# A sixth tile over VectorE and DRAM, and the norm weights moved ahead of the root, in a hybrid decoder layer

## The chip, the cores and the metric

The kernel runs on one core of one Trainium2 chip. The metric is the device time of one execution in microseconds; the kernel before took 946.97 us (median of three runs, 946.80 to 948.84). A profile is one execution recorded by the hardware; its times are us from the first instruction.

## The reference

One decoder layer over 1024 tokens of width 1024 (16 learned tokens go ahead of them and are dropped at the end), all in fp32:

```python
u = rmsnorm(h, g_pre_mix)
q, k, v, xr, yr = split(u @ w_in)
attn = sliding_window_attention_with_sinks(q, k, v, sinks)      # window 128
rec = gelu(yr) * rg_lru(causal_depthwise_conv(xr), ...)
h = h + rmsnorm(concat([attn, rec]) @ w_out, g_post_mix)        # first residual
u = rmsnorm(h, g_pre_ffn)                                       # second norm
f = square(relu(u @ w_ff1)) @ w_ff2                             # width 4096 inside
h = h + rmsnorm(f, g_post_ffn)
# rmsnorm(x, g) = x * rsqrt(mean(x * x) + 1e-6) * g
```

The change touches the two lines from the out-projection's norm to the second norm.

## The kernel before, in words

Every fp32 product is made of three matmuls: each operand is split into a high part, rounded to TensorE's fp32r format, and a low part, the rest (`split`: ScalarE casts, L96, VectorE subtracts, L99), and `mm3` (L125, L130, L131) adds high x high, high x low and low x high in a PSUM bank. The two products of the feed-forward part are done by a seven-product block scheme on halves of tokens, rows and columns, so that sums and differences of the normed rows (`t_sums`, `t_rest`) and of the weights (`prep_a`) are made beforehand on VectorE (`combine`, L1124).

The **out-projection** works on eight tiles of 128 tokens. `out_mm` adds eight chunks (`kc`) of 128 rows of `w_out` into two banks of 512 columns for each tile. For tiles 0 to 3 chunks 0 to 3 come first, then 4 and 5, then 6 and 7 tile by tile; tiles 4 to 7 run whole. After each tile `out_norm` does the first norm and residual:

- ScalarE squares both banks with a running sum (L1055) into `h` as scratch; VectorE adds the sums (L172), GpSimd takes the power -1/2 (L176): the root `rs`.
- VectorE multiplies each bank by `rs` and the weights `gmix_b` into `h` (L1061), then adds the residual `xr` (L1064). `h` goes to `out` (L1065).
- ScalarE squares `h` into `xr` as scratch (L1067), and GpSimd makes the second root `rs2`.

The second norm's rows must stand transposed, with features on the partitions, in the tiles `u2f` (`c` in the trace). There are two ways, and `MOVED` divides them:

- **Tiles below `MOVED`** (0 to 4): `u2_store` multiplies `h` by `rs2` and the weights `gpre_b`, reading both with a step of four elements so that the columns are "dealt" into four groups (L1011), transposes blocks of 32 x 32 on VectorE (L1018), and stores the tile to DRAM (L1019; `u_dram` in the trace). `u2_read` brings it back in four DMAs with the rows in place (L1023).
- **Tiles from `MOVED` on** (5 to 7): `out_scale` multiplies by `rs2` (ScalarE, L1081; tile 7 VectorE, L1079), and `u2_tiles` transposes eight blocks on TensorE against the identity (L1093) into two PSUM banks of tag `o`; ScalarE writes them to `u2f` times the norm weight by partition (L1110; half of tile 7 on VectorE, L1101).

Behind tile 7 TensorE goes straight on with the first products of the feed-forward part: `p1` and `p2` on tiles 0 to 3, then those that need all eight tiles (`ot2`, made by `t_sums`). `t_sums` is called three times: for tiles 4 and 5 (`slice(0, 8)`), then 6, then 7.

Buffers go by tags with a fixed count: `raw` 2 (`h`, early weights), `e` 2 (`gmix_b`, the transposed `y`, some weights), `d` 4 (`xr`), `ws` 5 (`gpre_b`, weights). A new user waits until the last one of a buffer is done. The order of instructions in each engine's queue is made by a scheduler that goes by program order as priority and by its own estimate of when operands and buffers are ready; `behind(a, b)` pins single instructions. Each queue, SyncE's DMA queue too, is worked off in order.

Of the kernel before, what the change touches and what calls it, by code (L numbers as in the profile page):

```python
# [11 lines left out]
AF = mybir.ActivationFunctionType  # L12
ALU = mybir.AluOpType
# [3 lines left out]
P = 128  # L17
D = 1024
# [19 lines left out]
def hybrid_layer(  # L38
# [6 lines left out]
    nc = tc.nc  # L45
# [12 lines left out]
    def slot(tag, shape, dt=F32):  # L58
        uid[0] += 1
        return slab.tile(shape, dt, tag=tag, name=f"{tag}{uid[0]}", bufs=bufs[tag])  # L60
# [20 lines left out]
    def lut(*args, **kwargs):  # L81
        ins = nc.scalar.activation(*args, **kwargs).ins
        if last_lut[0] is not None:
            tc.add_manual_dep(
                ins, last_lut[0],
                mybir.DependencyInfo(
                    mybir.DependencyClass.NoSync, mybir.DependencyReason.DATA
                ),
                reason="lut",
            )  # L90
        last_lut[0] = ins.name
        return ins
# [13 lines left out]
    def behind(name, *inss):  # L106
        for ins in inss:
            tc.add_manual_dep(
                ins, name,
                mybir.DependencyInfo(  # L110
                    mybir.DependencyClass.NoSync, mybir.DependencyReason.DATA
                ),
                reason="order",
            )
# [52 lines left out]
    def rstd_of(ssq_parts, n=P):  # L167
        ms = small.tile([P, 1], F32, name="ms", tag="ms")
        if len(ssq_parts) == 1:
            nc.gpsimd.tensor_scalar(ms[:n], ssq_parts[0], EPS, None, op0=ALU.add)  # L170
        else:
            nc.vector.scalar_tensor_tensor(  # L172
                ms[:n], ssq_parts[0], EPS, ssq_parts[1], op0=ALU.add, op1=ALU.add
            )
        rs = small.tile([P, 1], F32, name="rs", tag="rs")
        last_pow[0] = nc.gpsimd.tensor_tensor(  # L176
            rs[:n], ms[:n], half_pow[:n], op=ALU.pow
        ).ins.name
        return rs[:n]
# [50 lines left out]
    RMS_SC = 1.0 / math.sqrt(D)  # L230
# [744 lines left out]
    for half in range(2):  # L975
        for c in range(NLRU):
            y = ys[c][:, 512 * half : 512 * half + 512]
            ins = lut(y, y, AF.Gelu_apprx_tanh)
# [18 lines left out]
    gmix_b = slot("e", [P, D])  # L997
    nc.scalar.dma_start(gmix_b, g_post_mix[0].partition_broadcast(P))
    t4_dram = dpool.tile([P, 2, 4, 512], F32, name="t4_dram")

    MOVED = 5
    u2f = [[slot("c", [P, 16, 2, 32]) for _ in range(4)] for _ in range(2)]
    u2_dram = dpool.tile([MOVED, 4, P, 2 * P], F32, name="u2_dram")
    gpre_b = slot("ws", [P, D])
    nc.scalar.dma_start(gpre_b, g_pre_ffn[0].partition_broadcast(P))

    def dealt(t_):
        return t_.rearrange("p (n b) -> p b n", b=4)

    def u2_store(t, h, rs, tmp):  # L1010
        ins = nc.vector.scalar_tensor_tensor(  # L1011
            tmp.rearrange("p (b n) -> p b n", b=4), dealt(h), rs,
            dealt(gpre_b), op0=ALU.mult, op1=ALU.mult,
        ).ins
        if t < 3:
            behind(summed[t + 1], ins)
        y = slot("e", [P, D])
        nc.vector.transpose(y, tmp)  # L1018
        nc.sync.dma_start(u2_dram[t].rearrange("a (d b) r -> (a d) (b r)", b=4), y)  # L1019

    def u2_read(t):
        for q in range(4):
            nc.sync.dma_start(  # L1023
                u2f[t // 4][q][:, 4 * (t % 4) : 4 * (t % 4) + 4].rearrange(
                    "p a k t -> p a (k t)"
                ),
                u2_dram[t, :, :, 64 * q : 64 * q + 64].rearrange("a p r -> p a r"),
            )

    def out_mm(t, po, kcs):  # L1030
        half, o = t // 4, (t % 4) * P
        s = slice(o, o + P)
        for n in range(2):
            c = slice(512 * n, 512 * n + 512)
            for kc in kcs:
                ah, al = at[half][kc // 2]
                mm3(
                    po[n], (ah[:, kc % 2, s], al[:, kc % 2, s]),
                    (wo[kc][0][:, c], wo[kc][1][:, c]), kc == 0, kc == KC - 1,
                )  # L1040

    def out_banks(t):
        tag = ("pt", "o", "acc", "s", "pt", "acc", "s", "pt")[t]
        return [bank(tag), bank(tag)]

    summed = {}

    def out_norm(t, po):
        xr = slot("d", [P, D])
        nc.sync.dma_start(xr, x[t * P : (t + 1) * P, :])  # L1050
        h = slot("raw", [P, D])
        ssq = [small.tile([P, 1], F32, name=f"sq{n}", tag=f"sq{n}") for n in range(2)]
        for n in range(2):
            c = slice(512 * n, 512 * n + 512)
            nc.scalar.activation(  # L1055
                h[:, c], po[n], AF.Square, scale=RMS_SC, accum_out=ssq[n]
            )
        rs = rstd_of(ssq)
        for n in range(2):
            c = slice(512 * n, 512 * n + 512)  # L1060
            nc.vector.scalar_tensor_tensor(  # L1061
                h[:, c], po[n], rs, gmix_b[:, c], op0=ALU.mult, op1=ALU.mult
            )
        summed[t] = nc.vector.tensor_tensor(h, h, xr, op=ALU.add).ins.name  # L1064
        nc.sync.dma_start(out[t * P : (t + 1) * P, :], h)  # L1065
        ssq2 = small.tile([P, 1], F32, name="ssq", tag="ssq")
        squared[0] = nc.scalar.activation(  # L1067
            xr, h, AF.Square, scale=RMS_SC, accum_out=ssq2
        ).ins.name
        return h, xr, rstd_of([ssq2])  # L1070
# [3 lines left out]
    def out_scale(t, h, xr, rs2):  # L1074
        if t < MOVED:
            u2_store(t, h, rs2, xr)
            return None
        if t == 7:
            nc.vector.tensor_scalar(xr, h, rs2, None, op0=ALU.mult)  # L1079
        else:  # L1080
            nc.scalar.activation(xr, h, AF.Copy, scale=rs2)  # L1081
        return xr
# [4 lines left out]
    def u2_tiles(t, xn):  # L1087
        o = 4 * (t % 4)
        for k4 in range(0, KC, 4):
            pt = bank("o", (P, 4, P))  # L1090
            for i in range(4):
                kc = k4 + i
                turned[0] = nc.tensor.transpose(  # L1093
                    pt[:, i, :], xn[:, kc * P : (kc + 1) * P], ident
                ).ins.name
            pt = pt.rearrange("p k (a t) -> p k a t", t=32)
            for i in range(0, 4, 2):
                kc = k4 + i
                dst = by_k(u2f[1][kc // 2][:, o : o + 4])
                if k4 and t == 7:  # L1100
                    nc.vector.tensor_tensor(  # L1101
                        dst, pt[:, i : i + 2],
                        g_ffn_col[:, kc : kc + 2].rearrange(
                            "p (k a t) -> p k a t", a=1, t=1
                        ).to_broadcast([P, 2, 4, 32]),
                        op=ALU.mult,
                    )
                    continue
                for n in range(2):
                    ins = nc.scalar.activation(  # L1110
                        dst[:, n], pt[:, i + n], AF.Copy,
                        scale=g_ffn_col[:, kc + n : kc + n + 1],
                    ).ins
                    if t == 6:
                        behind(squared[0], ins)
# [137 lines left out]
    for t in range(8):  # L1253
        po = pos[t] if t < 4 else out_banks(t)
        out_mm(t, po, range(6 if t < 4 else 0, KC))
        if t > MOVED + 1:
            u2_tiles(t - 2, xns[t - 2])
        if t == 7:
            t3 = [slot("a", [P, 16, 2, 32]) for _ in range(2)]
            t2 = [slot("a", [P, 16, 2, 32]) for _ in range(2)]  # L1260
            ot2 = [pair("b", [P, 2, 512]) for _ in range(2)]
        halfway[t] = out_norm(t, po)
        for k in scale_at[t]:
            xns[k] = out_scale(k, *halfway.pop(k))
        if 1 <= t <= MOVED:
            u2_read(t - 1)
        if t == 7:
            t_sums(slice(0, 8))
            u2_tiles(6, xns[6])
        if t == 4:  # L1270
            a11_early.update(early(0, 0, pair("a", ESH)))
        if t == 5:
            b11 = operand(u2f[0][0:2])
            a12_early.update(early(1, 0, pair("ws", ESH)))
        if t == 6:
            b21 = operand(u2f[0][2:4])
            hl = slot("b", ESH, F32R), slot("e", ESH, F32R)
            a11_early.update(early(0, 2, hl))
# [375 lines left out]
```

## Time and profile before

| | before |
|---|---|
| median of three runs | 946.97 us |
| the profiled execution's own time | 947.39 us |
| its span, first to last instruction | 945.6 us |
| TensorE busy (matmul) | 936.1 us, 99% |
| VectorE busy | 663.6 us, 70% |
| ScalarE busy | 506.4 us, 54% |
| mean DMA rate over the span | 144 GB/s |
| granted TensorE clock | 0.998 |

How to read it: PE is TensorE, PEld its weight loads, DVE VectorE, ACT ScalarE, POOL GpSimd, SP SyncE, which here issues most DMAs. In a view by stages each entry is busy us of an engine in that stretch and, in brackets, the number of its instructions. In a timeline a line begins with the start and the duration; in brackets at its end stand the idle time of the engine before it and what ended it. In a view by lines a group has total busy us, mean ns of one, then idle time ahead of it. Matmuls overlap, so TensorE's speed is read from the starts of its instructions, not from its busy time.

### The profile page before, as it was taken

How to read it: one execution, taken by the hardware profiler on the slowest of the kernel's cores; microseconds unless marked ns; L12 is line 12 of the kernel's file. 1: busy time of each engine (PE TensorE's matmuls, PEld its weight loads, DVE VectorE, ACT ScalarE, POOL GpSimd, SP SyncE). 2: the span in 40 equal slices, each digit the busy share in tenths (PEclk: the TensorE clock that was granted, in tenths of full speed). 3: DMA queues.
4: the chain of work that ended last, by engine and by line, in shares of the span. 5: the costliest groups of instructions: out<-in, count | busy, mean ns of one | idle time of the engine just before them, and what ended most of it. 6: DMA issues, size and time to landing. Idle time of an engine off the chain costs nothing.

```text
span 945.6 us, 12176 instructions
## 1 busy us (share of the span) xinstructions
PE 936.1 (99%) x4576; PEld 783.4 (83%) x4576; DVE 663.6 (70%) x843; ACT 506.4 (54%) x847; POOL 134.1 (14%) x205
## 2 busy tenths in 40 slices
PE   9999999999999999999999999999999999999996
PEld 8999999877888888888888888888888888888885
DVE  6667788889977986755544465476667676779883
ACT  7546766579534864443655575654533443445441
POOL 4104436421021100110000000001111000001201
PEclk9999999999999999999999999999999999999999
DMA  9221011104259768574422364334787756547924
GB/s 273 58 52 39 24 46 40 51 23 134 93 186 299 222 196 281 184 251 135 156 89 89 113 217 120 107 112 113 199 170 172 213 179 193 187 133 208 242 62 89
DMA packets 99623, 135.96 MB, mean 144 GB/s; under 512 B 24359, under 2 KB 63287, under 8 KB 99565
## 3 DMA queue, kind: packets, MB, share of 16 engines
q1 hardware_dynamic: 90252, 109.69, 36.6%
q0 software_dynamic: 8880, 24.19, 12.1%
q10 hardware_dynamic: 432, 1.31, 0.4%
q8 instruction: 36, 0.59, 0.3%
q14 instruction: 23, 0.18, 0.1%
HBM read 113.08 MB, written 21.50 MB: 142 GB/s over the span
## 4 chain that ended last, share of the span: by engine, by line
PE 98%; DVE 1%; issue 0%; ACT 0%; DVEq 0%
PE ps_acc L125 11%; PE ps_acc L131 11%; PE ps_acc L130 11%; PE ps_pt L130 7%; PE ps_pt L125 7%; PE ps_pt L131 7%; PE ps_s L125 6%; PE ps_s L131 6%; PE ps_s L130 6%; PE ps_o L125 5%; PE ps_o L130 5%; PE ps_o L131 5%; PE ps_o L699 2%; PE ps_acc L924 1%; PE ps_s L629 1%; PE ps_s L633 1%
## 5 line engine op out<-in xcount | busy, mean ns | idle before, releaser
L99 DVE TENSOR_TENSOR ws<-raw,ws 128x1024 fp32r<-128x1024 f32 (+1 forms) x69 | 83.1, 1204 | 73.1 <-ACT ws L96 23.6
L96 ACT CAST ws<-raw 128x1024 fp32r<-128x1024 f32 (+1 forms) x68 | 69.7, 1026 | 83.1 <-PE ps_o L130 33.1
L96 ACT CAST ws<-e 128x1024 fp32r<-128x1024 f32 x41 | 43.0, 1049 | 85.1 <-PE ps_o L130 37.8
L99 DVE TENSOR_TENSOR b<-b,b 128x1024 fp32r<-128x1024 f32 (+1 forms) x49 | 57.5, 1176 | 27.6 <-PE ps_o L130 22.3
L130 PE MATMUL ps_acc<-a,ws 128*128 128x512 f32 (+3 forms) x224 | 76.3, 341 | 0.0
L125 PE MATMUL ps_acc<-a,ws 128*128 128x512 f32 (+3 forms) x224 | 76.3, 341 | 0.0
L131 PE MATMUL ps_acc<-a,ws 128*128 128x512 f32 (+3 forms) x224 | 75.7, 338 | 0.0
L96 ACT CAST b<-b 128x1024 fp32r<-128x1024 f32 (+1 forms) x49 | 49.5, 1011 | 41.7 <-DVE b L1124 35.5
L99 DVE TENSOR_TENSOR ws<-e,ws 128x1024 fp32r<-128x1024 f32 x41 | 50.1, 1222 | 29.6 <-ACT ws L96 16.6
L686 POOL TENSOR_SCALAR_AFFINE_SELECT c<-c 128x512 fp32r<-128x512 f32 x64 | 53.1, 845 | 73.6 <-ACT c L96 64.6
L131 PE MATMUL ps_acc<-ws,b 128*128 128x512 f32 (+1 forms) x120 | 46.1, 384 | 0.0
L130 PE MATMUL ps_acc<-ws,b 128*128 128x512 f32 (+1 forms) x120 | 46.1, 384 | 0.0
L125 PE MATMUL ps_acc<-ws,b 128*128 128x512 f32 (+1 forms) x120 | 46.0, 385 | 0.0
L125 PEld LDWEIGHTS ps_acc<-a,ws 128*128 128x128 f32 x224 | 42.2, 188 | 3.1 <-DVE b L933 0.3
L131 PEld LDWEIGHTS ps_acc<-a,ws 128*128 128x128 f32 x224 | 42.2, 188 | 3.0
L130 PEld LDWEIGHTS ps_acc<-a,ws 128*128 128x128 f32 x224 | 42.1, 188 | 2.8
L125 PE MATMUL ps_pt<-ws,b 128*128 128x512 f32 x112 | 44.2, 395 | 0.0
L130 PE MATMUL ps_pt<-ws,b 128*128 128x512 f32 x112 | 44.2, 394 | 0.0
L131 PE MATMUL ps_pt<-ws,b 128*128 128x512 f32 x112 | 44.0, 393 | 0.0
L125 PE MATMUL ps_s<-ws,b 128*128 128x512 f32 x110 | 43.5, 395 | 0.0
L130 PE MATMUL ps_s<-ws,b 128*128 128x512 f32 x110 | 43.3, 393 | 0.0
L131 PE MATMUL ps_s<-ws,b 128*128 128x512 f32 x110 | 43.2, 393 | 0.0
(423 smaller groups left out, 2682.8 us busy)
## 6 DMA issues: line engine op xcount, KB each, us to landing
raw<-in_w_ff_dram SPq DMA_DIRECT2D x59, 512.0 KB, 4.0
e<-in_w_ff_dram SPq DMA_DIRECT2D x43, 512.0 KB, 3.4
a<-in_w_ff_dram SPq DMA_DIRECT2D x12, 512.0 KB, 5.6
s_dram<-a POOLq DMA_DIRECT2D x12, 512.0 KB, 3.9
raw<-in_w_in_dram SPq DMA_DIRECT2D x9, 512.0 KB, 3.8
c<-in_x_dram SPq DMA_DIRECT2D x8, 512.0 KB, 5.3
d<-in_x_dram SPq DMA_DIRECT2D x8, 512.0 KB, 3.4
out_dram<-raw SPq DMA_DIRECT2D x8, 512.0 KB
```

The lines of the kernel that those rows point to most:

```text
L96: cast[0] = nc.scalar.copy(hi, src).ins.name
L99: low = nc.vector.tensor_tensor(lo, src, f32(hi), op=ALU.subtract).ins
L125: ins = nc.tensor.matmul(dst, lh, rh, start=start, stop=False, skip_group_check=True).ins
L130: nc.tensor.matmul(dst, lh, rl, start=False, stop=False, skip_group_check=True)
L131: last_mm[0] = nc.tensor.matmul(dst, ll, rh, start=False, stop=stop, skip_group_check=True).ins.name
L629: nc.tensor.matmul(dst, q[h][:, c], hi, start=True, stop=False, skip_group_check=True,)
L633: nc.tensor.matmul(dst, q[h][:, c], lo, start=False, stop=True, skip_group_check=True,)
L686: nc.gpsimd.affine_select(out=p_[:, :, s], in_=f32(p_[:, :, 0]), pattern=[[0, 4], [g, P]], compare_op=op, fill=0.0, base=0, channel_multip ...
L699: nc.tensor.matmul(two[:, :, oc : oc + w], v, p_.rearrange("p (j i) s c -> p j (i s c)", j=2)[:, :, pc : pc + w], start=n == 0 and k == 0, ...
L924: ins = nc.tensor.matmul(y2_bank[half], (wh, wh, wl)[k][:, kc, :], (uh, ul, uh)[k][:, t0 : t0 + n], start=m % 24 == 0, stop=m % 24 == 23, ...
```

## The change

Three things are changed together. `MOVED` becomes 6, so tile 5 takes the way over VectorE and DRAM, and `u2_tiles` is called for tiles 6 and 7 alone. In `u2_store` ScalarE scales `h` by `rs2` and deals the columns in the same instruction, and VectorE multiplies the dealt rows in place by weights that ScalarE has dealt once beforehand (`gpre_n`, in a buffer of tag `e`, to `gpre_b`). In `out_norm` VectorE multiplies the banks by `gmix_b` into `h` first; ScalarE squares the banks in place behind that; and one instruction on VectorE multiplies `h` by the root and adds the residual.

```diff
-    MOVED = 5
+    MOVED = 6
...
-    gpre_b = slot("ws", [P, D])
-    nc.scalar.dma_start(gpre_b, g_pre_ffn[0].partition_broadcast(P))
+    gpre_n, gpre_b = slot("e", [P, D]), slot("ws", [P, D])
+    nc.scalar.dma_start(gpre_n, g_pre_ffn[0].partition_broadcast(P))
...
+    nc.scalar.copy(gpre_b.rearrange("p (b n) -> p b n", b=4), dealt(gpre_n))
+
     def u2_store(t, h, rs, tmp):
-        ins = nc.vector.scalar_tensor_tensor(
-            tmp.rearrange("p (b n) -> p b n", b=4), dealt(h), rs,
-            dealt(gpre_b), op0=ALU.mult, op1=ALU.mult,
-        ).ins
+        nc.scalar.activation(
+            tmp.rearrange("p (b n) -> p b n", b=4), dealt(h), AF.Copy, scale=rs
+        )
+        ins = nc.vector.tensor_tensor(tmp, tmp, gpre_b, op=ALU.mult).ins
         if t < 3:
             behind(summed[t + 1], ins)
...
         for n in range(2):
             c = slice(512 * n, 512 * n + 512)
+            nc.vector.tensor_tensor(h[:, c], po[n], gmix_b[:, c], op=ALU.mult)
             nc.scalar.activation(
-                h[:, c], po[n], AF.Square, scale=RMS_SC, accum_out=ssq[n]
+                po[n], po[n], AF.Square, scale=RMS_SC, accum_out=ssq[n]
             )
         rs = rstd_of(ssq)
-        for n in range(2):
-            c = slice(512 * n, 512 * n + 512)
-            nc.vector.scalar_tensor_tensor(
-                h[:, c], po[n], rs, gmix_b[:, c], op0=ALU.mult, op1=ALU.mult
-            )
-        summed[t] = nc.vector.tensor_tensor(h, h, xr, op=ALU.add).ins.name
+        summed[t] = nc.vector.scalar_tensor_tensor(
+            h, h, rs, xr, op0=ALU.mult, op1=ALU.add
+        ).ins.name
```

## The prediction

> **What bounds the kernel now.** I read the page's busy shares and its chain of work first, then the busy time by stages, then single rows of TensorE.
>
> ```profile
> PE 936.1 (99%) x4576; PEld 783.4 (83%) x4576; DVE 663.6 (70%) x843; ACT 506.4 (54%) x847; POOL 134.1 (14%) x205
> PE 98%; DVE 1%; issue 0%; ACT 0%; DVEq 0%
> ```
> ```profile
> core 0: us, PE busy (x) PEld busy (x) DVE busy (x) ACT busy (x) POOL busy (x), PEclk, DMA share, GB/s
> 210.00:240.00 30.00, 30.00 (x133) 23.42 (x130) 28.80 (x26) 29.57 (x35) 3.40 (x3) 1.00 0.41 123
> 240.00:268.80 28.80, 28.80 (x126) 23.34 (x125) 22.18 (x28) 11.85 (x22) 1.88 (x4) 1.00 0.27 92
> 268.80:313.26 44.46, 44.46 (x194) 35.99 (x193) 36.29 (x37) 19.86 (x38) 8.45 (x15) 1.00 0.84 260
> 313.26:335.35 22.09, 22.09 (x109) 18.32 (x108) 21.04 (x37) 17.87 (x44) 3.70 (x6) 1.00 0.80 243
> 275.00:305.00 30.00, 30.00 (x132) 24.32 (x131) 24.41 (x24) 10.27 (x22) 5.97 (x11) 1.00 0.98 298
> 305.00:315.00 10.00, 10.00 (x49) 8.25 (x48) 8.25 (x9) 8.28 (x16) 0.55 (x1) 1.00 0.62 187
> ```
>
> The chain is TensorE for 98% of the span. A busy PE need not be a fast one, so I count: 125 weight loads in 28.80 us are one matmul each 0.230 us, and 130 in 30.00 or 193 in 44.46 are the same pace, with the clock at 1.00. So through the whole out-projection, up to 313 us, TensorE is fed without a hole. Two things follow. First, a shorter norm on VectorE and ScalarE buys nothing by itself, since nobody on the chain waits for it. Second, the change can gain only what it takes out of TensorE's own queue; it can lose wherever it makes TensorE wait. VectorE is close behind: 21.04 of 22.09 us between 313.26 and 335.35. The DMA engines are as full, 0.98, from 275 to 305.
>
> **What leaves TensorE.** Tile 5's eight transposes.
>
> ```profile
> 313.02 0.39 PE L131 MATMUL ps_pt<-a,b 128*128 128x512 f32 x1
> 313.26 1.03 PE L1093 MATMUL ps_o<-ident,d 128*128 128x128 f32 x8
> 314.05 0.48 PE L125 MATMUL ps_acc<-b,a 128*128 128x512 f32 x1
> 314.36 0.39 PE L130 MATMUL ps_acc<-b,a 128*128 128x512 f32 x1
> ```
>
> From the first transpose to the second matmul behind them are 314.36 - 313.26 = 1.10 us; one matmul of pace 0.23 belongs to the stream anyway, so the block costs 0.87 us. Bounds: the bare step from 313.26 to 314.05 is 0.79; eight times a transpose's whole duration would be more, as priced among the rivals. I take 0.87, because it counts the late start of the next matmul as well.
>
> **What VectorE and ScalarE do instead.** All eight tiles change in their norm, and six (before: five) go over DRAM.
>
> ```profile
> L1011 DVE SCALAR_TENSOR_TENSOR d<-raw,rs,ws 128x1024 f32<-128x1024 f32 x5 | 10.3, 2066 | 1.1 <-POOL rs L176 1.1
> L1064 DVE TENSOR_TENSOR raw<-raw,d 128x1024 f32<-128x1024 f32 x8 | 9.8, 1223 | 0.2
> L1018 DVE STREAM_TRANSPOSE e<-d 128x1024 f32<-128x1024 f32 x5 | 6.2, 1242 | 0.1
> L1061 DVE SCALAR_TENSOR_TENSOR raw<-ps_pt,rs,e 128x512 f32<-128x512 f32 x6 | 4.2, 747 | 1.9 <-POOL rs L176 1.9
> L1244 DVE TENSOR_TENSOR b<-ps_pt,b 128x512 f32<-128x512 f32 x2 | 1.4, 687 | 0.2 <-PE ps_pt L131 0.2
> ```
> ```profile
> L871 DVE SCALAR_TENSOR_TENSOR c<-b,c 128x1040 f32<-128x1040 f32 x4 | 4.9, 1233 | 1.0 <-ACT c L82 1.0
> ```
> ```profile
> L1067 ACT ACTIVATE d<-raw 128x1024 f32<-128x1024 f32 x8 | 8.6, 1069 | 21.1 <-DVE raw L1064 15.8 <-issue 5.3
> L1110 ACT ACTIVATE c<-ps_o,gcol 128x128 f32<-128x128 f32 x20 | 5.5, 383 | 2.1 <-PE ps_o L1093 2.1
> L96 ACT CAST a<-raw 128x1024 fp32r<-128x1024 f32 x5 | 5.2, 1041 | 1.4 <-DMA raw<-in_w_ff_dram 1.4
> L1081 ACT ACTIVATE d<-raw,rs 128x1024 f32<-128x1024 f32 x2 | 2.3, 1152 | 1.0 <-POOL rs L176 1.0
> ```
>
> VectorE: the dealing multiply of 2.07 us (L1011) becomes a plain in-place product, 1.22 by L1064: five times -0.85 is -4.2. The bank products go from 0.75 to 0.69 (L1244 reads a bank too), sixteen times -0.06 is -1.0. The sum becomes a SCALAR_TENSOR_TENSOR, 1.23 by L871 at 1040 elements against 1.22: nothing. Tile 5 adds a product and a transpose, 1.22 + 1.24 = +2.5. Net -2.7 us, on an engine that isn't on the chain.
>
> ScalarE: five new scalings by L1081, +5.8; one dealing of the weights, +1.0 by L96; tile 5's eight evictions go, which with their overlap are 2.2 us of the stage (row below); tile 5's own scaling stays. Net +4.6, beside 24.6 idle us between 268.80 and 313.26. The new scalings read every fourth element, and no ScalarE row does that. VectorE's rows bound it: L1011 with such reads takes 2.07 where L871, the same operation without, takes 1.23, a factor of 1.68. So a scaling lies between 1.15 and 1.93; I take 1.15 for the sum, the engine's own row, and keep 1.93 for the range. At 1.93 six of them add 4.7 us, still in idle time, and each tile's rows are 0.8 later. The Trainium skill (SBUF — State Buffer, Door 1: The DMA port swizzle) says that SBUF works in 16-byte lines and needs two hits on a line for full rate, so a step of four fp32 values pays on every access. By that rule the upper end is the right one; the L1011 row agrees with it, and the end of the kernel would be the same by either.
>
> Order on the engines: the squares now wait for the bank product, 0.69 more ahead of the root, but behind the root only 1.23 is left instead of 2 x 0.75 + 1.22 = 2.7. The sum of a tile comes 0.8 us sooner. In front of the squares VectorE now also carries the wait for a raw buffer that ScalarE carried; behind it on VectorE stand the products and transposes of the tile before, as they stood behind the sums.
>
> **What is late next.** TensorE reaches the first product that needs the last transposed tile 0.87 us earlier:
>
> ```profile
> 334.60 0.76 DVE L99 TENSOR_TENSOR b<-a,b 128x256 fp32r<-128x256 f32 x2
> ```
> ```profile
> 335.35 0.39 PE L125 MATMUL ps_acc<-b,e 128*128 128x512 f32 x1
> 335.59 0.39 PE L130 MATMUL ps_acc<-b,e 128*128 128x512 f32 x1
> ```
>
> The two low halves come at about 335.0 and 335.4; the first is read at 335.59, the second some six matmuls later. Cover: about 0.6 us, less than the 0.87 taken away, so VectorE must finish 0.3 us sooner to let the gain through. It should: tile 7's squares stood behind the evictions that go.
>
> ```profile
> 313.89 2.18 ACT L1110 ACTIVATE c<-ps_o,gcol 128x128 f32<-128x128 f32 x8 [1.72 <-PE ps_o L1093]
> 316.95 0.64 ACT L1055 ACTIVATE raw<-ps_pt 128x512 f32<-128x512 f32 x1
> ```
>
> Tile 7's products ended near 313.3, its squares began at 316.95. With 2.2 us off ScalarE and 1.5 less behind the root, 0.3 is there.
>
> **Sum.** The profiled execution took 947.39 us for a span of 945.6, so 1.8 lie around the span; it stands 0.42 above the median of the runs, 946.97. Span: 945.6 - 0.87 = 944.7, with what lies around it 946.5; on the median 946.97 - 0.87 = **946.1 us**, -0.09%. About 0.2%, 1.9 us, is what a measurement of this kernel can tell from no change, so this counts as the same.
>
> **Rivals.**
>
> *Tile 5's rows land late, and VectorE stands (slower).* Tile 5's half of the operand was written from PSUM by 316.1; now it takes the way of tile 4:
>
> ```profile
> 291.57 1.22 DVE L1064 TENSOR_TENSOR raw<-raw,d 128x1024 f32<-128x1024 f32 x1
> 300.74 1.23 DVE L1064 TENSOR_TENSOR raw<-raw,d 128x1024 f32<-128x1024 f32 x1
> 301.88 1.24 DVE L1018 STREAM_TRANSPOSE e<-d 128x1024 f32<-128x1024 f32 x1
> 316.18 0.68 DVE L1124 TENSOR_TENSOR a<-c,c 128x512 f32<-128x512 f32 x1
> ```
> ```profile
> 303.73 0.38 SPq L1019 DMA_DIRECT2D u_dram<-e  x1
> 308.05 2.52 SPq L1023 DMA_DIRECT2D c<-u_dram  x4
> DMA to landing us min/median/max: 2.9/3.6/4.8
> ```
> ```profile
> 290.81 0.39 PE L131 MATMUL ps_acc<-a,b 128*128 128x512 f32 x1
> 297.17 0.60 ACT L1055 ACTIVATE raw<-ps_acc 128x512 f32<-128x512 f32 x1 [0.74 <-DVE d L1011]
> 304.19 1.15 ACT L1081 ACTIVATE d<-raw,rs 128x1024 f32<-128x1024 f32 x1 [0.99 <-POOL rs L176]
> ```
>
> Tile 4's sum ended at 292.8, its store was issued at 303.7, its four reads by 310.6, and they landed near 314.2: 21.4 us. The same lag from tile 5's sum at 302.0 gives 323.4, 7.2 us behind the instruction at 316.18 that reads these rows (t_sums). VectorE's queue is in order: behind it stand tile 7's norm, the early weight products and the rest of that operand, which have 0.6 us of cover. At the full 7.2 TensorE ends 6.6 late: 953.6. Against it: much of tile 4's lag was no transfer. Its transpose ran only at 301.88, nine us behind its sum. Without that wait, from a sum to its store are 2.2 us to the scaling (302.0 to 304.19, tile 5's squares and root), 1.15 for it, 1.22, 1.24 and some 0.4 for the issue, 6.2 in all; from store to landing 10.5 as above. With 16.7 us tile 5 lands at 302.0 - 0.8 + 16.7 = 317.9. Its norm took 4.8 us from 297.17, though its products had ended at 291.2; started then, and 0.8 shorter, its sum is there at 295.2 and its rows at 311.9. So it decides at about 316.8, in the middle of what I can bound. What speaks for it besides is the DMA: 0.98 busy at 298 GB/s, and tile 5 brings 0.5 MB out and 0.5 MB in, 3.5 us at that rate, ahead of weights in the same SyncE queue; the reads also stand in that queue until the store has landed. The Trainium skill (DMA: Bandwidth & Descriptors, Where 436 GB/s comes from) puts the HBM side of one core at about 358 GB/s; the 298 of the row lies under it, with the engines full. I price the middle, 3 to 4 us late, less the 0.6: about **950**.
>
> *The gain is eaten.* VectorE doesn't finish sooner, and the 0.87 is waited off at 335.35: 947.0. Or the dealing of the weights (1.04 to 1.75) falls into 210 to 240 us, where ScalarE is busy 29.57 of 30.00 and VectorE 28.80, so that a delay can reach TensorE: 946.1 + 1.04 = 947.1, at most 947.9.
>
> *More comes off than counted.* If a transpose cost its whole 272 ns (this row's mean), eight would be 2.2 us: 944.8. The step of 0.79 speaks against it, and the pace leaves no other hole to close.
>
> ```profile
> L1093 PE MATMUL ps_o<-ident,d x24: 270/272/273, 313.3 to 331.1; 128*128 128x128 f32 x24
> ```
>
> **Chances.** Forecast 0.40; gain eaten 0.15; rows late by enough to exceed 0.2% 0.38; more than counted 0.07. So faster 0.07, same 0.55, slower 0.38. The two signs share it, so the forecast's own range is 945.8 to 946.6 (0.79 to 1.03 us off, and 0.2 of scatter). For 8 in 10 it goes up into the late rows: 945.5 to 952.0, which leaves out the 0.07 below and about 0.1 of the latest landings.
>
> **What would show it.** Right: sixteen transposes in place of 24, TensorE's pace at 0.230 through 345 us, tile 5's reads landed before VectorE's first t_sums, the scaling at 1.15. Wrong: idle time of VectorE ahead of t_sums with a DMA as releaser, or of TensorE near 320 to 345; a copy of the weights among ScalarE's work before 244 with TensorE's pace broken there; a start later than 313 us of the first early product.

## The result, and the profile after

| | before | after |
|---|---|---|
| median of five runs each | 946.80 us | 956.04 us |
| lowest to highest | 946.35 to 948.84 | 955.42 to 957.05 |
| the profiled execution's own time | 947.39 us | 955.42 us |
| its span | 945.6 us | 953.7 us |

The ratio is 1.0097, with a 95% interval of 1.0086 to 1.0108: slower by 9.2 us on the medians, 8.0 between the two profiled executions. The forecast of 946.1 and its whole range (945.5 to 952.0) lie below it; the likeliest case failed, and the late-rows rival was too cheap.

The page after, its busy line and the shares of its chain of work:

```profile
PE 937.6 (98%) x4568; PEld 783.7 (82%) x4568; DVE 660.0 (69%) x845; ACT 517.0 (54%) x845; POOL 131.4 (14%) x205
PE 85%; ACT 5%; DVE 4%; DMA 2%; issue 2%; SPq 1%; POOL 1%; DVEq 0%; ACTq 0%; POOLq 0%
```

There are eight TensorE instructions less, but its share of the chain fell from 98% to 85%: in places the chain now runs through other engines. TensorE's three largest waits after (us in total, times, longest) name the places; the first and the third are new:

```profile
PE ps_acc L125 <- ACT b L96: 4.3, 1, 4.3
PE ps_acc L309 <- DVE base_e L563: 1.5, 1, 1.5
PE ps_pt L125 <- ACT a L96: 1.5, 2, 0.8
```

**The first loss, at 226 and 233 us.** ScalarE's timeline after:

```profile
216.11 1.15 ACT L82 ACTIVATE b<-c,m8sp 128x1040 f32<-128x1040 f32 x1
217.16 2.05 ACT L1010 COPY ws<-e 128x1024 f32<-128x1024 f32 x1
219.12 1.16 ACT L82 ACTIVATE c<-c,m4sp 128x1040 f32<-128x1040 f32 x1
```

The weights' dealing has no idle time of ScalarE on either side of it. Everything behind it comes later, and TensorE waits twice for a cast of `w_out`: between the starts of neighbouring matmuls lie 1236 and 1071 ns in place of 230.

```profile
225.86 0.40 PE L125 MATMUL ps_o<-ws,b 128*128 128x512 f32 x1
227.10 0.74 PE L125 MATMUL ps_pt<-a,b 128*128 128x512 f32 x2 [0.84 <-ACT a L96]
234.54 0.50 PE L125 MATMUL ps_pt<-a,b 128*128 128x512 f32 x1 [0.67 <-ACT a L96]
```

**The second loss, at 335 us.** TensorE and VectorE after, on tile 5's way and at the operand `ot2`:

```profile
301.47 1.28 DVE L1062 SCALAR_TENSOR_TENSOR raw<-raw,rs,d 128x1024 f32<-128x1024 f32 x1 [0.67 <-POOL rs L176]
302.68 1.24 DVE L1020 STREAM_TRANSPOSE e<-d 128x1024 f32<-128x1024 f32 x1
307.09 1.23 DVE L1016 TENSOR_TENSOR d<-d,ws 128x1024 f32<-128x1024 f32 x1 [3.18 <-ACT d L1013]
313.97 1.24 DVE L1020 STREAM_TRANSPOSE e<-d 128x1024 f32<-128x1024 f32 x1
315.24 0.33 SPq L1021 DMA_DIRECT2D u_dram<-e  x1
318.79 1.99 SPq L1025 DMA_DIRECT2D c<-u_dram  x3
323.07 0.69 DVE L1124 TENSOR_TENSOR a<-c,c 128x512 f32<-128x512 f32 x1 [2.20 <-DMA c<-u_dram]
325.63 1.28 DVE L1062 SCALAR_TENSOR_TENSOR raw<-raw,rs,d 128x1024 f32<-128x1024 f32 x1
```
```profile
335.68 0.40 PE L131 MATMUL ps_pt<-b,a 128*128 128x512 f32 x1
340.37 0.79 PE L125 MATMUL ps_acc<-b,e 128*128 128x512 f32 x1 [4.29 <-ACT b L96]
340.96 0.78 PE L130 MATMUL ps_acc<-b,e 128*128 128x512 f32 x1
```

Tile 5's sum is done at 302.75, its product waits for ScalarE's scaling until 307.09, its transpose (the second of the two L1020) comes at 313.97, its store at 315.24, its reads by 320.8. VectorE stands 2.20 us ahead of its first `t_sums` with a DMA as releaser, the sign that the prediction named for its rival; tile 7's sum (the last VectorE row) stands behind it. TensorE then stops for 4.69 us from start to start. The releaser named there is ScalarE's cast of `ot2`, but that cast itself stood waiting for VectorE's sums. After:

```profile
339.91 0.40 ACT L96 CAST b<-a 128x256 fp32r<-128x256 f32 x1 [2.36 <-DVE a L1124]
```

and before, for the casts at the same place:

```profile
334.15 1.70 ACT L96 CAST b<-a 128x256 fp32r<-128x256 f32 x3 [0.29 <-DVE a L1124]
```

**The third loss, behind it.** TensorE by stretches of 3.41 us after (busy us, instructions, granted clock):

```profile
core 0: us, PE busy (x), PEclk, DMA share, GB/s
336.12:339.53 3.41, 0.00 (x0) 1.00 0.00 0
339.53:342.94 3.41, 2.57 (x6) 0.50 0.86 272
342.94:346.35 3.41, 3.41 (x10) 0.50 0.10 36
346.35:349.76 3.41, 3.41 (x17) 1.00 0.01 2
```

From 339.53 on the granted clock is 0.50 for 6.8 us. TensorE works from 340.37, so 6.0 us of work go at half speed: about 3.0 us lost. Before, the clock stayed at 1.00 there.

Added up on the spans: the steps at 226 and 233 cost 1.0 + 0.8, the stop 4.69 - 0.23 = 4.5, the clock 3.0, and eight transposes give 0.87 back: 8.4, against 953.7 - 945.6 = 8.1.

### The profile page after: what moved, and what is told of

Read it like the earlier page. It is cut to its first block, busy times and chain, and to the rows that moved or that the text cites. A ratio compares the mean times of both kernels' runs of the same rounds, so it can differ in the third digit from the quotient of the medians.

```text
span 953.7 us, 12154 instructions
## 1 busy us (share of the span) xinstructions
PE 937.6 (98%) x4568; PEld 783.7 (82%) x4568; DVE 660.0 (69%) x845; ACT 517.0 (54%) x845; POOL 131.4 (14%) x205
## 4 chain that ended last, share of the span: by engine, by line
PE 85%; ACT 5%; DVE 4%; DMA 2%; issue 2%; SPq 1%; POOL 1%; DVEq 0%; ACTq 0%; POOLq 0%
PE ps_acc L125 10%; PE ps_acc L130 10%; PE ps_acc L131 10%; PE ps_s L131 6%; PE ps_s L130 6%; PE ps_s L125 6%; PE ps_pt L125 5%; PE ps_pt L130 5%; PE ps_pt L131 5%; PE ps_o L130 5%; PE ps_o L131 5%; PE ps_o L125 5%; PE ps_o L699 2%; ACT c L82 1%; DMA c<-in_x_dram 1%
## 5 line engine op out<-in xcount | busy, mean ns | idle before, releaser
L99 DVE TENSOR_TENSOR ws<-raw,ws 128x1024 fp32r<-128x1024 f32 (+1 forms) x69 | 83.0, 1204 | 69.2 <-PE ps_o L130 23.0
L99 DVE TENSOR_TENSOR b<-b,b 128x1024 fp32r<-128x1024 f32 (+1 forms) x49 | 57.6, 1176 | 27.6 <-PE ps_o L130 22.3
L99 DVE TENSOR_TENSOR ws<-e,ws 128x1024 fp32r<-128x1024 f32 x41 | 50.1, 1222 | 28.0 <-ACT ws L96 14.6
```

The costliest lines, as they stand in the source:

```text
L99: low = nc.vector.tensor_tensor(lo, src, f32(hi), op=ALU.subtract).ins
```

## The experiments

All medians stand beside runs of the kernel before on the same chip, which took 946.4 to 947.0. Two limits on what they can tell: the intervals of runs with four executions are some 1.6 us wide to either side, and the traces differ by up to 1.4 us before anything that is changed begins (the same matmul starts at 215.40 us in the kernel before and at 214.02 in the run with the load alone). Differences of about 1 us between such runs stay open. The theory after this reading: (1) the copy of the weights costs 1.5 us; (2) tile 5's late rows hold VectorE, and TensorE waits for the operand; (3) the clock adds some 3 us to a long stop. Rivals: ScalarE's strided scaling, the reordered norm, or VectorE's load by itself.

**Five tiles, all else as changed**

```diff
-    MOVED = 6
+    MOVED = 5
```

> The change with five tiles through DRAM in place of six; the rest of it stays (ScalarE scales and deals, the weights are dealt by ScalarE's copy, the norm is reordered). Late rows: tile 5 is turned on TensorE again, so VectorE has no landing to wait for ahead of t_sums, TensorE has no idle time near 335 us and its clock no stretch at 0.5; what is left is the copy of the weights, some 1.5 us at 226 and 233 us: 946.8 + 1.5 = 948.3, between 947.8 and 949. Rival, the slow strided scaling of ScalarE (2.13 us where 1.15 was taken) alone delays the norms: still idle between 320 and 345 us and over 951. Rival, the late rows are all of it: 946.8.

948.78 us, 1.0019 (1.0010 to 1.0029). No stop at 335 (longest step 0.49 us), clock 1.00 throughout, the steps at 226 and 233 still there (1.21 and 1.10 us). So the sixth tile holds some 7.3 of the 9.2 us.

**The sixth tile alone**, in the kernel before: `MOVED = 6` and nothing else.

> The kernel before with six tiles through DRAM and nothing else: VectorE still scales and deals, the norm keeps its order, no copy of the weights. Late rows: tile 5's rows land after VectorE's t_sums want them (316 us in the trace of before), VectorE stands there, TensorE stands near 335 us for 3 to 5 us, and its clock falls to 0.5 for some 7 us after it; no steps at 226 and 233 us: 951 to 955, the middle 946.8 - 0.9 + 4.5 + 2.8 = 953. Rival, it is ScalarE's strided scaling that makes the rows late: then VectorE's dealing keeps them in time, and 946 to 947.

955.65 us, 1.0095 (1.0078 to 1.0111). VectorE deals, no weights are copied, the norm keeps its order, and it is as slow. The strided scaling on ScalarE is not needed for the loss. Its VectorE timeline:

```profile
299.60 1.23 DVE L1064 TENSOR_TENSOR raw<-raw,d 128x1024 f32<-128x1024 f32 x1
303.06 2.12 DVE L1011 SCALAR_TENSOR_TENSOR d<-raw,rs,ws 128x1024 f32<-128x1024 f32 x1 [1.08 <-POOL rs L176]
311.65 1.24 DVE L1018 STREAM_TRANSPOSE e<-d 128x1024 f32<-128x1024 f32 x1
322.13 0.69 DVE L1124 TENSOR_TENSOR a<-c,c 128x512 f32<-128x512 f32 x1
```

Dealt by 305.2, turned only at 311.65, behind the splits' subtractions (L99) and tile 6's bank products. TensorE's longest step is 3.58 us, its clock 0.50 for 6.8 us.

**The reordered norm alone**, in the kernel before

```diff
-            nc.scalar.activation(h[:, c], po[n], AF.Square, ..., accum_out=ssq[n])
+            nc.vector.tensor_tensor(h[:, c], po[n], gmix_b[:, c], op=ALU.mult)
+            nc.scalar.activation(po[n], po[n], AF.Square, ..., accum_out=ssq[n])
...
-        summed[t] = nc.vector.tensor_tensor(h, h, xr, op=ALU.add).ins.name
+        summed[t] = nc.vector.scalar_tensor_tensor(
+            h, h, rs, xr, op0=ALU.mult, op1=ALU.add).ins.name
```

> The kernel before with the reordered norm alone (weights multiply the banks ahead of the root, the squares stay in PSUM, one last instruction multiplies by the root and adds). Theory that the norm has no part in the loss: 946.8, within 0.5; each tile's sum is there up to 0.8 us sooner, which nothing on TensorE's path uses. Rival, the squares stand behind something new (the products read the same banks) and the norms of tiles 5 to 7 come later: over 948, with idle time of TensorE near 335 us.

948.01 us, 1.0011 (1.0002 to 1.0020), so 1.1 us slower: just at the rival's bound, and with the idle time near 335 us that the rival named. Two steps appear at the operand:

```profile
334.40 0.40 PE L131 MATMUL ps_pt<-b,a 128*128 128x512 f32 x1
335.36 0.49 PE L125 MATMUL ps_acc<-b,e 128*128 128x512 f32 x1 [0.56 <-ACT b L96]
336.19 0.50 PE L130 MATMUL ps_acc<-b,e 128*128 128x512 f32 x1 [0.34 <-DVE b L99]
```

Between 310 and 326 us VectorE waits longer than before: 0.9 for a cast and 0.8 for ScalarE's squares, neither among its waits before. So a norm that takes less work left `ot2` later: the squares now stand behind VectorE's product.

**The weights dealt by GpSimd**

```diff
-    nc.scalar.copy(gpre_b.rearrange("p (b n) -> p b n", b=4), dealt(gpre_n))
+    nc.gpsimd.tensor_copy(gpre_b.rearrange("p (b n) -> p b n", b=4), dealt(gpre_n))
```

> The change with the weights dealt by GpSimd's copy in place of ScalarE's. Theory that ScalarE's 2.05 us copy at 217 us costs TensorE its steps of 1236 and 1071 ns at 226 and 233 us: both go back to the pace and the time falls by 1.5 us, from 956.0 to 954.5; the idle time near 335 us stays. Rival, those steps come from something else, or what is saved there is waited off at 335 us, since tile 5's rows land when they land: 956.0 unchanged.

955.22 us, 1.0091 (1.0076 to 1.0106). The steps at 226 and 233 are gone, and a step of 2.10 us stands at 218.6 in their place. VectorE and GpSimd there:

```profile
217.02 3.07 DVE L854 TENSOR_TENSOR b<-b,b 128x1040 f32<-128x1040 f32 x1
216.08 2.90 POOL L1010 COPY ws<-e 128x1024 f32<-128x1024 f32 x1
```

The VectorE instruction beside GpSimd's copy takes 3.07 us; in the change it took 1.23. TensorE waits for the VectorE copy behind it (L933). The 0.8 us by which the median lies under the change's is within the scatter.

**The weights dealt later on ScalarE**

```diff
-    nc.scalar.copy(gpre_b..., dealt(gpre_n))
+    behind(cast[0], nc.scalar.copy(gpre_b..., dealt(gpre_n)).ins)
```

> The change with ScalarE's copy of the weights ordered behind ScalarE's last cast of the recurrent half (near 240 us), where ScalarE has idle time, in place of 217 us. Theory that a copy anywhere in 210 to 240 us costs TensorE about 1.5 us: no step over 0.5 us between 220 and 240, and 956.0 - 1.5 = 954.5. Rival, everything after it is paced by tile 5's landing and the gain is waited off at 335 us: 956.0, with a longer wait there (near 6 us).

954.64 us, 1.0084 (1.0068 to 1.0101), 1.4 less than the change. The copy runs at 255.5, and between 220 and 240 no step is over 0.5 us. So the copy was what made the steps at 226 and 233. What it costs in time is less clear: the intervals of this run and of the change overlap (1.0068 to 1.0101, 1.0086 to 1.0108), and TensorE now stops at three later places, 1.8 us at 328, 3.2 at 337 and 1.5 at 361, more in all than the one stop of 4.69 us.

**The stop filled with work**

```diff
+        if p == 0:
+            spare = bank("o")
+            for _ in range(18):
+                behind(last_mm[0], nc.tensor.matmul(spare, ..., start=True, stop=True).ins)
         product(ya[p], wa[p][1], ot2, False)
```

> The change with 18 matmuls more (operands at hand, a bank that nobody reads, their result unused), placed on TensorE where it waits near 335.7 us; 18 x 0.231 = 4.2 us of its 4.46 us of waiting are filled, and nothing else is touched. Theory that the 4.7 us step is what takes the clock to 0.5 for 6.8 us, and that this costs 2.8 us beside the wait: clock 1.0 through, matmuls at 0.231 behind it, 956.0 - 2.8 = 953.2. Rival, the clock falls for another reason or costs nothing that is not hidden: 956.0.

953.60 us, 1.0073 (1.0057 to 1.0089), 2.4 less than the change, by adding work. The clock is 1.00 throughout. So the fall of the clock comes from the stop, as (3) says; its price is known roughly, since the four runs lie between 952.09 and 954.99, and the profiled one is the slowest of them.

**Tile 5's landing taken away**: its reads fetch tile 4's rows once more, as many transfers, and tile 5's part of the second norm is left out of the result.

```diff
-                u2_dram[t, :, :, 64 * q : 64 * q + 64]...
+                u2_dram[min(t, 4), :, :, 64 * q : 64 * q + 64]...
```

> The change, but the read of tile 5 takes tile 4's rows out of DRAM once more: as many transfers, none of which waits for tile 5's own turning and store (the sixth tile's part of the second norm is left out of the result so). Theory that the landing of tile 5's rows is what delays: VectorE has no idle time ahead of t_sums for a DMA, t_sums start before 319, TensorE has no step over 1.5 us near 335 and its clock stays at 1.0: 956.0 - 4.5 - 2.8 = 948.7, between 947.8 and 950. Rival, VectorE is late with tile 6's and tile 7's norms by itself (tile 7's sum at 326.9 in the change, 322.65 before): the wait stays over 2 us and the time over 952.

952.78 us, 1.0062 (1.0044 to 1.0080): 3.3 less than the change, where theory (2) asked for 7.3. VectorE no longer waits for rows, and `t_sums` follow tile 6's sum at once:

```profile
316.95 1.28 DVE L1062 SCALAR_TENSOR_TENSOR raw<-raw,rs,d 128x1024 f32<-128x1024 f32 x1 [0.66 <-POOL rs L176]
318.16 0.68 DVE L1124 TENSOR_TENSOR a<-c,c 128x512 f32<-128x512 f32 x1
```
```profile
335.43 0.40 PE L131 MATMUL ps_pt<-b,a 128*128 128x512 f32 x1
338.56 0.50 PE L125 MATMUL ps_acc<-b,e 128*128 128x512 f32 x1 [2.74 <-ACT b L96]
```

Yet TensorE stops for 3.1 us, and its clock falls for 3.4. The landing is about a third of the loss, not all of it. Theory (2) fell in this form, and the rival's signs came (a wait over 2 us, a time over 952). The theory for what was left: VectorE's own load.

**The same, and tile 5 not dealt at all** (its part of the second norm is left out here too)

```diff
+        if t == 5:
+            return None
         if t < MOVED:
             u2_store(t, h, rs2, xr)
```

> As v_read4 (tile 5's read takes tile 4's rows), and tile 5's scaling, product, turning and store are left out too (its part of the second norm is left out of the result). Theory that what is left in v_read4 is VectorE's added work in 302 to 316 us (product 1.23, transpose 1.24, and the wait for the scaling ahead of them): TensorE has no step over 1 us near 335 and the time is 946.8 + 1.5 (copy) - 0.87 (eight transposes) + 0 to 1.1 (reordered norm) = 947.4 to 948.5. Rival, the norms of tiles 6 and 7 are late by themselves with the reordered norm: over 951.

948.83 us, 1.0019 (1.0009 to 1.0028), 3.95 less than with the landing alone taken away, and as fast as five tiles, though 0.3 over the range that was expected. TensorE's steps are 1.05 and 0.83 us, at the same two instructions as with the norm alone:

```profile
335.81 0.50 PE L125 MATMUL ps_acc<-b,e 128*128 128x512 f32 x1 [0.66 <-ACT b L96]
336.65 0.50 PE L130 MATMUL ps_acc<-b,e 128*128 128x512 f32 x1 [0.34 <-DVE b L99]
```

**Only the load, in the kernel before**

```diff
+        if t == 5:
+            y = slot("e", [P, D])
+            nc.vector.transpose(y, xr)
+            nc.vector.tensor_tensor(y, y, gpre_b, op=ALU.mult)
         return xr
```

> The kernel before with two instructions more on VectorE, one transpose and one product of 128x1024 on tile 5's scaled rows (2.5 us, result unused), in the queue where the change has them. Theory that VectorE's queue between tile 5's norm and the operand at 335 us has only 0.6 us of cover: TensorE waits 1.9 us near 335: 946.8 + 1.9 = 948.7, and up to 1.7 more if its clock falls for one stretch of 3.4 us: 948 to 950.5. Rival, VectorE's idle time there (3.4 us of the 10 us from 300) takes them in: 946.8.

950.42 us, 1.0037 (1.0023 to 1.0050). Two VectorE instructions, 2.5 us, no DMA, no change of the norm. The transpose ran at 310.75 and the product at 313.67, so near the change's places (307.09 and 313.97), not at them:

```profile
333.76 0.40 PE L131 MATMUL ps_pt<-b,a 128*128 128x512 f32 x1
336.03 0.65 PE L125 MATMUL ps_acc<-b,e 128*128 128x512 f32 x1 [1.87 <-ACT b L96]
```
```profile
332.79:336.20 3.41, 1.54 (x7) 1.00 0.86 280
336.20:339.61 3.41, 3.41 (x8) 0.50 0.00 0
```

TensorE waits 1.87 us, 2.5 less the 0.6 of cover, and the clock falls for 3.4 us: 1.9 + 1.7 = 3.6, measured 3.8. VectorE's 3.2 idle us near 303, which are there before as well, took nothing in: they are the wait for tile 5's own root and ScalarE's work behind it, and the added work comes after them.

**One run instead of steps in tile 5's scaling**, on top of the landing taken away, with the same part left out of the result

```diff
+        if t == 5:
+            nc.scalar.activation(tmp, h, AF.Copy, scale=rs)
```

> As v_read4, with tile 5's scaling on ScalarE read and written in one run of 1024 instead of 256 by 4 (tile 5's part is left out of the result as there). Theory that the strided scaling's length stands in VectorE's queue ahead of the early casts: it goes from 2.13 to 1.15, VectorE's idle time ahead of tile 5's product from 3.2 to 2.2, the step at 335 shrinks by about 1.0 us: 952.8 - 1.0 = 951.8, or 950 if the clock keeps its rate. Rival, the casts wait for other things: 952.8.

952.18 us, 1.0050 (1.0034 to 1.0065), 0.6 less, which these runs do not tell from nothing. In the profiled execution tile 5's product and transpose run 2.0 us sooner, but VectorE then waits 1.6 us for casts, and TensorE's step is 2.89 instead of 3.13. The clock stays at 1.00 there, and a new step of 1.75 us stands at 357.7, so what one place gave back another took.

**Attempts at the order: a second place for y, later sums**

```diff
-        y = slot("e", [P, D])
+        y = slot("e" if t % 2 == 0 else "ws", [P, D])
```
```diff
-            t_sums(slice(0, 8))
+            t_sums(slice(0, 4))
...
-    t_sums(slice(8, 12))
+    t_sums(slice(4, 12))
```

> The change with the turned rows y in two places in turn (even tiles as now, odd tiles in a free slot of another tag), so that tile 5's transpose need not wait for tile 4's store. On VectorE it then stands ahead of two casts and of tile 6's bank products. Theory that one y buffer and VectorE's order make tile 5 late: transpose near 311 in place of 313.97, store near 312, landing near 321, VectorE's idle time ahead of t_sums down from 2.7 to under 0.5 us, TensorE's step of 4.69 us shrunk to under 2, clock 1.0 through: 956.0 - 4.46 + 1 - 2.8 = 949.7, between 948.5 and 951. Rival, the transfers (not the transpose) set the landing: it stays near 324.9 and the time over 954.

956.01 us, 1.0104 (1.0088 to 1.0120). A miss. Tile 5 was turned at 311.40 in place of 313.97, but its reads were issued at 316.5, 3.9 us after its store, with two loads of weights just ahead of them in SyncE's queue; its norm also came later. VectorE no longer waited for rows, and TensorE's step was still 4.25 us.

> Both edits together: the copy of the weights behind ScalarE's last cast of the recurrent half, and y in two places. If the two costs add: 949.7 - 1.5 = 948.2, between 946.5 and 949.5. If the 1.5 us saved ahead only make TensorE come 1.5 us sooner to the same late operand, as rows and sums cannot move with it: 949.7 or more.

954.32 us, 1.0083 (1.0068 to 1.0098), no different from the later copy by itself.

> The change with t_sums called for tile 4 alone where it was called for tiles 4 and 5, and for tiles 5 and 6 together after the early products; the rows land when they land, but VectorE is not queued behind the landing with tile 7's norm. Theory that VectorE's standing in order (2.2 + 0.5 us) is most of the loss: TensorE's step of 4.69 shrinks by about 2.7 to 2.0 us, and a wait so short leaves the clock at 1.0: 956.0 - 2.7 - 2.8 = 950.5, at worst 953.3 with the clock as before. Rival, the chain from the landing to the last of these sums is what ends late: 956 and no shorter wait.

955.47 us, 1.0089 (1.0071 to 1.0107), with a step of 5.26 us. A miss: the sums of tile 5 come later by the new order than by the wait.

> The kernel before with six tiles through DRAM and y in two places in turn; VectorE still scales and deals. In the run with six tiles alone, tile 5 was dealt by 305.2 but turned only at 311.65, stored at 312.9 and landed at 321.9. Theory that for it the one y buffer and the order that follows from it are the delay: turned near 307, stored by 308.5, read by 312, landed near 317, t_sums near 317; TensorE's step at 334 under 1.5 us, clock 1.0: 946 to 948.5, middle 947. Rival, what VectorE is given to do in these 30 us is too much in any order: the step stays over 3 us, 953 to 956.

954.83 us, 1.0085 (1.0069 to 1.0101), a step of 3.37 us. Tile 5 was turned at 309.13, and `t_sums` still began only at 320.65.

> The same with t_sums split as well (tile 4 alone first, tiles 5 and 6 together after the early products), so that tile 7's norm does not stand behind tile 5's landing. If both edits work: no step over 0.5 us near 335, clock 1.0, eight transposes less on TensorE: 946.8 - 0.87 = 945.9, between 945.7 and 947.5. Rival, the sums of two tiles in one go come too late for the product at 335 us: 948 to 950.

957.19 us, 1.0107 (1.0091 to 1.0123), a step of 4.36 us: slower than either expectation.

None of these five finds an order in which the sixth tile fits, with or without the reordered norm.

**Five tiles and the later copy**

> The change with five tiles through DRAM and the copy of the weights at ScalarE's idle time. Theory that with five tiles the copy is most of what is left: 948.8 - 1.4 = 947.4, no step over 0.5 us between 220 and 240. Rival, TensorE's 1.5 us of delay at 226 and 233 give VectorE the time that it lacks at 335 us, and are waited off there: 948.8.

947.94 us, 1.0014 (1.0003 to 1.0024). Between the expectations, and not told from five tiles alone (1.0010 to 1.0029). The steps at 226 and 233 are gone. Seven of the ten runs took 946.5 to 948.3 us and three 949.7 to 950.1; the profiled one, at 950.07, is the slowest. In it TensorE, there sooner, stops 1.96 us at 333.8 with its clock at 0.50 for 3.4 us: what the copy had taken was waited off there, and more. That the quicker runs had no such fall is likely, but no trace shows it.

No kernel of these beats the one before. What the eight transposes can give is 0.87 us.

## Why the prediction was wrong

**What bounds the kernel** was right: TensorE is the chain, a shorter norm buys nothing, and the change loses wherever TensorE waits. It did, at two places.

**What leaves TensorE** (0.87 us): sixteen transposes remain, as said. The gain never arrived. With the landing and the dealing both away, the time was still that of five tiles.

**The dealing of the weights** was sized at 1.04, at most 1.75; it took 2.05. Its place was named among the rivals (1.0 to 1.8 us over the forecast, chance 0.15 with another), and there its cost came: 1.0 + 0.8 us in the trace. Moved to idle time it gave back 1.4 on the medians, at the edge of the scatter.

**The scalings** were taken at 1.15 with an end of 1.93:

```profile
L1013 ACT ACTIVATE d<-raw,rs 128x1024 f32<-128x1024 f32 x6 | 12.9, 2142 | 5.0 <-POOL rs L176 5.0
```

2.14 is over both. The prediction drew on VectorE's factor of 1.68; on ScalarE it is 2.142 / 1.152 = 1.86. By the Trainium skill (SBUF — State Buffer, Door 1: The DMA port swizzle), a step of four fp32 values pays on every access; the trace agrees that it pays, and the value should have been taken from the upper end. For the time it mattered little: no clear difference for tile 5, and six tiles dealt by VectorE are as slow.

**VectorE's net of -2.7 us**, and the 0.3 us sooner that was read from it, is the step that failed. The whole is right, even low: 663.6 to 660.0. But the sum ran over stages with different limits. The savings lay on tiles 0 to 4, where VectorE got idle time for them (24.41 busy us between 275 and 305 before):

```profile
275.00:305.00 30.00, 30.00 (x132) 24.34 (x131) 20.06 (x23) 17.23 (x28) 5.30 (x12) 1.00 1.00 301
```

The added 2.5 us for tile 5 lay between 307 and 315, at the head of the stretch to 335 in which the prediction itself had VectorE busy for 21.04 of 22.09 us, with a cover of 0.6 at its end. Set against that cover they are a loss of 1.9 us with no landing and no rival at all; the two added instructions in the kernel before showed this, with a wait of 1.87 us and 3.8 us in all. That VectorE "must finish 0.3 us sooner" and "should" rested on ScalarE's evictions that go and on 1.5 us less behind the root; the work that tile 5 adds to VectorE in the same stretch was not set against it.

**The late rows** (chance 0.38): the mechanism is there, with the sign that was asked for. The landing was put between 311.9 and 317.9; the reads were issued up to 320.8, and VectorE stood until 323.07. The step that failed is the transpose's time: "without that wait" counted the transpose straight behind the scaling, while it stood at 313.97, 5.7 us after its product, behind the splits' subtractions and tile 6's products. The 21.4 us lag of tile 4, set aside as mostly no transfer, was the better guide: its 323.4 is close to where VectorE stood. The price, 3 to 4 us less 0.6, is near the 3.3 that the landing gave back, but by luck: without the landing TensorE's step shrank by 1.6 us (4.69 to 3.13), and a shorter fall of the clock, which stood in no term, gave part of the rest.

**What the range lacked**: causes that come together, and the clock. Tile 5's landing 3.3, its own work on the engines 4.0 (956.04 - 952.78 and 952.78 - 948.83), and 2.0 for the copy and the norm, less a gain that never came: 9.2, each term good to about 1.5 us. Each was counted as a case of its own. The clock's part in them, 3.0 us by the trace and 2.4 by the run with the stop filled, stood in no term; the Trainium skill (TensorE: Matmul & The Clock Gate, HAM oscillation — how this bites in real kernels) warns of TensorE's idle stretches over some 3.4 us, and the stop of 4.69 agrees with it. The forecast's own upper end is off as well: 946.97 - 0.79 + 0.2 is 946.4, not 946.6, and no working is shown for the 1.03.

**The norm's sum 0.8 sooner per tile**: alone it cost 1.1 us. What it saves behind the root it takes in front of it, in VectorE's order.

## What to carry to other kernels

Sum an engine's savings and additions by stage, not over the kernel: microseconds saved where it idles do not pay for those added where it has 0.6 us of cover. When an instruction's inputs are ready says little about when it runs; count what stands ahead of it in its queue. Here the lag of the last like item was a better guess than the same lag with its waits taken out. And price a stop of TensorE with the clock that falls behind it: 2.5 us of VectorE work cost 3.8.

## What the runs showed of the hardware

**The granted clock goes by stretches of 3.4 us, and a stop shorter than one can take it down.** Wherever it fell between 200 and 400 us in these traces, it was 0.50 for either 3.4 or 6.8 us. The run with the later copy:

```profile
325.16:328.57 3.41, 3.41 (x19) 1.00 0.71 250
328.57:331.98 3.41, 1.77 (x11) 1.00 0.96 275
331.98:335.39 3.41, 3.41 (x11) 0.50 0.69 241
335.39:338.80 3.41, 2.12 (x9) 1.00 0.00 0
```

A stretch with 1.77 us of work, its longest step 1.81 us, was followed by one at half speed; a stretch with 2.12 us was not. Yet less work can pass, as in the run with the weights dealt by GpSimd:

```profile
333.27:336.69 3.42, 1.55 (x7) 1.00 0.01 2
336.69:340.10 3.41, 1.17 (x4) 1.00 0.54 165
340.10:343.51 3.41, 3.41 (x10) 0.50 0.43 143
```

Here 1.55 us was followed by full speed, and only the 1.17 us behind it by half. Over all traces, between 200 and 400 us and with the stretches laid off from where each trace's clock changed, every stretch at full speed with up to 1.45 us of work was followed by half speed, and none with over 1.9 us was. In between both happened: 1.54, 1.74, 1.77 and 1.85 us took the clock down, 1.55, 1.68, 1.79, 1.81 and 1.86 did not. So the work in a stretch does not decide alone; what else does stays open. The steps of 1.2 and 1.1 us at 226 and 233 never took it down. The Trainium skill (TensorE: Matmul & The Clock Gate, What's actually happening) speaks of free-running windows of 3413 ns and puts the half rate behind an idle one; the length agrees, but here less than half a window of idle time (3.41 - 1.77) was enough.

**A GpSimd copy slows VectorE beside it.** With GpSimd's strided copy running, a VectorE product of 1.23 us took 3.07. It ended at 220.09, 1.11 us behind the copy's end at 218.98, as if it had stood until then; GpSimd's spans are rough, though. The Trainium skill (Advanced Engine Details and Errata, VectorE Performance Modes, Mode Summary) says that VectorE's second port to SBUF is shared with GpSimd; that this is the cause here was not tried.

**ScalarE with a step of four fp32 values** took 2.05 (copy) and 2.14 us (scaling) for 1024 elements, against 1.15 for a scaling in one run of 1024 (1152 ns for tile 5, in the run that tried it).
